# One copy of k and v out of PSUM: who frees the projection's bank in a hybrid decoder layer

## The chip, the cores and the metric

The kernel runs on one core of one Trainium2 chip. The metric is the device time of one execution in microseconds, from the kernel's first to its last work on the chip. Lower is better. The kernel before was run three times.

## The reference

The reference is one layer of a decoder in float32, for a prompt of 2048 tokens (with 16 learned tokens ahead of it) and 32 sample tokens (8 sequences of 4). Cut to what matters here:

```python
def in_project(h, g_pre, w_in):
    hn = rmsnorm(h, g_pre)
    proj = jnp.einsum('bsd,de->bse', hn, w_in)      # 1280 columns
    ...
    return q, k, v, u                               # 512, 128, 128, 512 columns

q, k = partial_rope(q, pos_p), partial_rope(k, pos_p)   # the first 16 of 64 columns of each head are rotated
att_o = swa_prompt(q, k, v, attn_sinks[l])              # window 128, blocks of 128, 8 heads of q, 2 of k and v
ssm_o, hr, hi = ssm_mixer(u, None, None, *ssm_p)        # complex state space, 32 groups
hp = hp + merge_out(att_o, ssm_o, ...)
hp = hp + sqrelu_mlp(hp, ...)
```

`partial_rope` rotates columns 0 to 7 against 8 to 15 of each head: x1 cos - x2 sin and x2 cos + x1 sin. The outputs are the layer's result for both kinds of tokens, the last 128 rows of k (rotated) and v, and the states of the state-space group.

## The kernel before, in words

The kernel has four stages: the u projection of all tokens with the preparation of the state-space tables (`phase_u`, to about 160 us of the span), attention and state space together (`phase_att`), the gated unit and the output projection (`phase_mix`), and the MLP (`phase_mlp`). All products are float32 by three matmuls: each operand is split into a high half, rounded by a ScalarE copy (`ACT.activation(..., AF.Copy)` into a float32r tile), and a low half, the difference (`split`, L93 to L99, and `mm3`, L108).

`phase_att` (L719) walks over 16 blocks of 128 tokens, `for i in range(NT)` at L993. A pass does, in the program's order: the scores of block i in two halves (`scores`, matmuls at L819, mask and maximum on VectorE at L824, exponentials on ScalarE at L830), the transposes of block i + 1's q and k (`tr`), the q, k and v projection of block i + 2 (`qkv_mm`, L436 and L437), one pair of the state-space groups (`s_rot`, `s_split`, `s_scan`, `s_hsplit`, `s_out`, `s_in`), the normalisation of the probabilities (L843, L845), their transposes with the split into PTh and PTl (`ptrans`, L847), `rope(i + 2)` between the two, the products with v (`pv`, `mm3` on PTh, PTl and v), and the split of block i + 3's x into axh and axl (`split_x`, the low half on GpSimd, L739). While this runs, GpSimd forms sums of MLP weights in `sums_step` (L1476 to L1479).

`rope` (L748) runs 17 times: for the 16 blocks and once, early, for the 48 sample and learned tokens (`rope(NT)`). It takes the two PSUM banks of the projection, `pq` (512 columns of q) and `pkv` (128 of k, 128 of v), and does in the kernel before:

- on ScalarE (ACT): the copy of k into columns 512 to 639 of the tile `qk`, scaled by the token's norm (L754); the copy of q into the first 512 (L755); the copy of v out of PSUM into its high half `vh` in the tile `v` (L759);
- on VectorE (DVE): the product with the cosines into the tile `ra` (L764), two products with the sines into `rb` (L765, L766), the sum of both back into `qk` (L767), and v's low half from PSUM, `vl` = v times norm less `vh` (L768);
- for the last block and the sample tokens also a plain copy of v out of PSUM into `vraw` (L771), and two DMAs from GpSimd's queue that store v and k (L773, L774; L776, L777). For the sample tokens VectorE splits `vraw` into `vns` (L778, L779).

So the bank of `pkv` is read by L754, L759, L768 and at times L771, and it is free for its next user when the last of them has read it.

PSUM has six banks for `mm_bank` and one tile of two banks, `b`, that the state-space products share (`b2_bank`, bufs=1). `s_in` (L905, 12 matmuls by `mm3` on sxh and sxl) can only write `b` when `s_out`'s result has been copied out by ACT at L960 (`sy`), and `s_out` when `s_rot` has read it (L920 to L922, VectorE).

The order in which an engine does its instructions isn't the program's. The kernel is built with a planner that places the instructions of every engine with a simulated timeline (`schedule_with_timeline_sim=True`, L1768): an instruction that is ready early in that model can be put ahead of one that stands before it in the program. Each engine then does its own list in order, and waits on semaphores for the others.

Of the kernel before, what the change touches and what calls it, by code (L numbers as in the profile page):

```python
# [8 lines left out]
F32 = mybir.dt.float32  # L9
F32R = mybir.dt.float32r  # L10
BF16 = mybir.dt.bfloat16
AF = mybir.ActivationFunctionType
OP = mybir.AluOpType
# [40 lines left out]
def ap(t, offset, dims):  # L54
    return bass.AP(tensor=t.tensor, offset=t.offset + offset, ap=[list(x) for x in dims])
# [3 lines left out]
def hymba_step(ctx: ExitStack, tc: tile.TileContext, A, O):  # L59
    nc = tc.nc  # L60
    PE, ACT, DVE, POOL, SP = nc.tensor, nc.scalar, nc.vector, nc.gpsimd, nc.sync
# [4 lines left out]
    def pool(stack, name, **kw):  # L66
        return stack.enter_context(tc.tile_pool(name=name, bufs=1, reuse_waits="tile", **kw))
# [7 lines left out]
    def mm_bank():  # L75
        return PS["pool"].tile([128, 512], F32, tag="mm", name="mm", bufs=PS["mm"])
# [4 lines left out]
    def r(t):  # L81
        return t.bitcast(F32)
# [52 lines left out]
    rstd = cst.tile([128, NT + 1], F32, name="rstd")  # L135
# [20 lines left out]
    def w_rows(ap_, k, c0, n):  # L156
        return ap_[k * 128:(k + 1) * 128, c0:c0 + n]

    # ------------------------------------------------------------------ u projection
    class Paced:  # L160
        def __init__(self, eng):
            self.eng = eng
# [556 lines left out]
    def phase_att(outer, eq, qw, QP, X01):  # L719
        with ExitStack() as es:  # L720
            cs, masks = AC["cs"], AC["masks"]
            pw = pool(es, "aw")
            wk = pool(es, "awork")
# [3 lines left out]
            vr = [pw.tile([128, 4, 2, 192], F32R, name=f"v{n}") for n in range(2)]  # L727
# [14 lines left out]
            def slot(i):  # L742
                return (i if i < NT else 3) % 4
# [4 lines left out]
            def rope(i):  # L748
                pq, pkv = QP.pop(i)
                n = 128 if i < NT else NX  # L750
                t = wk.tile([128, 10, 64], F32, name="qk", tag="qk", bufs=2)
                QK[i] = t
                tf = t.rearrange("p h d -> p (h d)")
                ACT.activation(tf[:n, 512:640], pkv[:n, :128], AF.Copy, scale=rstd[:n, i:i + 1])  # L754
                ACT.activation(tf[:n, :512], pq[:n], AF.Copy, scale=rq[:n, i:i + 1])  # L755
                s = slot(i)
                vp = pkv[:n, 128:256].rearrange("p (k d) -> p k d", k=2)
                vh, vl = (vr[m][:n, s, :, 64:128] for m in range(2))
                ACT.activation(vh, vp, AF.Copy, scale=rstd[:n, i:i + 1])  # L759
                c = cs[:n, i, 0, None, :].to_broadcast([n, 10, 16])  # L760
                sn = cs[:n, i, 1, None, :].to_broadcast([n, 10, 16])
                a = wk.tile([128, 10, 16], F32, name="ra", tag="ra", bufs=1)
                b = wk.tile([128, 10, 16], F32, name="rb", tag="rb", bufs=1)
                DVE.tensor_tensor(a[:n], t[:n, :, 0:16], c, op=OP.mult)  # L764
                DVE.tensor_tensor(b[:n, :, 0:8], t[:n, :, 8:16], sn[:, :, 0:8], op=OP.mult)  # L765
                DVE.tensor_tensor(b[:n, :, 8:16], t[:n, :, 0:8], sn[:, :, 8:16], op=OP.mult)  # L766
                DVE.tensor_tensor(t[:n, :, 0:16], a[:n], b[:n], op=OP.add)  # L767
                DVE.scalar_tensor_tensor(vl, vp, rstd[:n, i:i + 1], r(vh), op0=OP.mult, op1=OP.subtract)  # L768
                if i >= NT - 1:
                    v = wk.tile([128, 128], F32, name="vraw")  # L770
                    ACT.activation(v[:n], pkv[:n, 128:256], AF.Copy, scale=rstd[:n, i:i + 1])  # L771
                    if i < NT:
                        POOL.dma_start(O["v_p"], v)  # L773
                        POOL.dma_start(O["k_p"], t[:, 8:10, :].rearrange("p h d -> p (h d)"))  # L774
                    else:
                        POOL.dma_start(O["v_s"][:, 124:128, :], v[:NS])  # L776
                        POOL.dma_start(O["k_s"][:, 124:128, :], t[:NS, 8:10, :].rearrange("p h d -> p (h d)"))  # L777
                        DVE.tensor_copy(vns[:, 0], v[:n])  # L778
                        DVE.tensor_tensor(vns[:, 1], v[:n], r(vns[:, 0]), op=OP.subtract)  # L779
# [93 lines left out]
                    ACT.dma_start(ATD[:, :, :, 16 * i:16 * i + 16].rearrange("p k s c -> p (k s) c"),  # L873
                                  at.rearrange("p (a c) -> p a c", c=16))

            # state space: one pair of groups per step
            SX, SC, SS, SH = {}, {}, {}, {}
            wz = [pw.tile([128, 2, 2, 192], F32R, name=f"wz{n}") for n in range(2)]
            hst = pw.tile([128, 2, NCY], F32, name="hst")
# [101 lines left out]
            split_x(2)  # L981
            qkv(0)
            rope(0)
            tr(0)
            rope(NT)
            s_load(1)
            s_split(0)
            s_in(0)
            qkv(1)
            tr(NT)  # L990
            rope(1)
            nxt = 0
            for i in range(NT):  # L993
# [67 lines left out]
                load_a(i)  # L1061
                proj_a(i)

    # ------------------------------------------------------------------ gated unit, sample attention, output projection
    def advance(gen, n=1):
        for _ in range(n):
            next(gen, None)
# [101 lines left out]
        return 128 if i < NT else NS  # L1169

    def squares(pl, x, p, parts):
        """sums of squares over the four channel tiles: [channel, token]"""
        q = pl.tile([128, 4, 128], F32, name="pq", tag="pq", bufs=1)
        for k, s_ in parts:
            ACT.activation(q[:, k:k + s_.shape[1], :p], s_, AF.Square)
        q2 = pl.tile([128, 2, 128], F32, name="pq2", tag="pq2", bufs=1)
        POOL.tensor_tensor(q2[:, :, :p], q[:, 0:2, :p], q[:, 2:4, :p], op=OP.add)
        q3 = pl.tile([128, 128], F32, name="pq3", tag="pq3", bufs=2)
        POOL.tensor_tensor(q3[:, :p], q2[:, 0, :p], q2[:, 1, :p], op=OP.add)
        return q3  # L1180
# [216 lines left out]
        turn(ORD[NT])  # L1397
        return pre

    # ------------------------------------------------------------------ MLP  # L1400
    # Both products are cut in halves along tokens, contraction and result (Strassen-Winograd): seven products
    # of quarters each, with the sums of the activations' quarters formed in place and those of the weights' once.
    HN = (336, 352, 352)
    COL0 = (0, 672, 1376)
    ORDER = {"u": (1, 4, 6, 7, 5, 2, 3), "d": (4, 1, 6, 7, 5, 2, 3)}
# [82 lines left out]
    def phase_mlp(pre):  # L1488
        with ExitStack() as es:
# [5 lines left out]
            def add(out, a, b):  # L1495
                DVE.tensor_tensor(out, a, b, op=OP.add)  # L1496

            def combine(p, n, pt, q, both):
                """C11 = P1 + P2, C12 = P1 + P6 + P5 + P3, C21 = P1 + P6 + P7 - P4, C22 = P1 + P6 + P7 + P5"""
                if p == 1:  # L1500
                    ACT.activation(q[0], pt, AF.Copy)
                elif p == 4:
                    ACT.activation(q[2], pt, AF.Copy, scale=-1.0)
                elif p == 6:
                    add(q[1], q[0], pt)
                elif p == 7:
                    add(q[3], q[1], pt)
                    add(q[2], q[2], q[3])
                elif p == 5:
                    add(both, both, pt[:, None, :].to_broadcast([128, 2, n]))  # L1510
                elif p == 2:
                    add(q[0], q[0], pt)
                else:
                    add(q[1], q[1], pt)
# [31 lines left out]
                    combine(p, n, ACC["t"][t], q, Y[:, 4 + t, :2 * n].rearrange("p (i c) -> p i c", i=2))  # L1546

            def rows(c, p):
                """runs of up to 128 columns that hold tokens of one kind: (first column, number, rows of the output)"""
                out = []  # L1550
                while p:
                    j, x = divmod(c, 128)
                    n = min(p, 128 - x)
                    if j < NT:
                        r0 = 1024 * (j % 2) + j // 2 + 8 * x
                        dst = ap(O["y_p"], r0 * D, [[8 * D, n], [1, D]])
                    else:
                        dst = O["y_s"][x:x + n]
                    out.append((c, n, dst))
                    c, p = c + n, p - n  # L1560
                return out
# [35 lines left out]
                        end_b(*x, pt, c)  # L1597

            def end_a(c, n):
                """the first half of the features of the last tokens, scaled by the gain"""  # L1600
                f = M["H"].rearrange("p a c -> p (a c)")
                i = len(END)
                o = f[:, 1024 * i:1024 * i + 1024]
                h1 = f[:, 1024 * i + 3072:1024 * i + 4096] if i < 2 else mw.tile([128, D], F32, name="h1", tag="h1", bufs=1)
                SP.dma_start(h1[:n], H1D[COL0[2] + c:COL0[2] + c + n])
                st = mw.tile([128, 8], F32, name="est", tag="est", bufs=3)
                pt = mm_bank()[:n]
                for k in range(4):
                    PE.transpose(pt[:, 128 * k:128 * k + 128], Y[:, k, c:c + n], ident)
                sq = mw.tile([128, 512], BF16, name="esq", tag="esq", bufs=1)  # L1610
                ACT.activation(sq[:n], pt, AF.Square, accum_out=st[:n, 0:1])
                DVE.tensor_tensor(o[:n, :512], pt, gpost[:n, :512], op=OP.mult)
                END.append((o, h1, st))
# [159 lines left out]
```

## Time and profile before

| what | value |
|---|---|
| runs of the kernel before | 2208.49, 2202.45 and 2210.93 us, median 2208.49 us |
| span of the profiled execution | 2198.8 us, 37175 instructions |
| the profiled execution's own time | recorded by its span alone |
| PE (matmul) busy | 2083.1 us, 95% of the span |
| DVE, ACT, POOL busy | 1645.6, 1324.0 and 397.2 us |
| mean granted clock of PE | 0.970 of full speed |

PE is TensorE, DVE VectorE, ACT ScalarE, POOL GpSimd. The span goes from the first to the last instruction of one execution. "Busy" is the time in which an engine has an instruction under way; matmuls overlap, and their ends are modelled. A granted clock of 1.00 is the upper of TensorE's two levels, 2.4 GHz, and 0.50 the lower, 1.2 GHz. Busy shares over the whole span mix stages with different limits, so the tables that matter below are those of one stage.

### The profile page before, as it was taken

Reading aid. Unit: us, or ns where it says so; the run is one execution under the profiler, and the core shown is the slowest. Engines: PE = TensorE matmul, PEld = TensorE weight load, DVE = VectorE, ACT = ScalarE, POOL = GpSimd, SP = SyncE. Lnnn points to the kernel's source line nnn. Section 1 sums busy time; section 2 is a strip of 40 time slices with the busy share of each in tenths; the row PEclk is TensorE's granted clock in tenths of the full one; section 3 lists DMA queues with packets and bytes.
Section 4 is the critical chain, followed back from the end, with each engine's and each line's share of the span. In section 5 each row is a group of like instructions: output and inputs, shape, how many; then the busy total and the mean of one; then the engine's idle time right before and its main releaser. Section 6 shows DMA issues by size and latency. Waiting matters only on the chain.

```text
span 2198.8 us, 37175 instructions
## 1 busy us (share of the span) xinstructions
PE 2083.1 (95%) x12968; PEld 1963.3 (89%) x12968; DVE 1645.6 (75%) x3412; ACT 1324.0 (60%) x2877; POOL 397.2 (18%) x435
## 2 busy tenths in 40 slices
PE   7888999997799999989999999999999999999997
PEld 7877888786678787889999999999999999999995
DVE  8947788788678647469896885787868757787686
ACT  6644655555665545537865555588555555875555
POOL 5513545455142334000000000000000000000001
PEclk9998999998899999999999999999999999999999
DMA  8894666655577526778745465454454564444554
GB/s 291 240 222 117 158 183 169 166 155 158 168 224 256 184 85 209 221 240 287 246 144 144 136 189 184 139 191 135 137 143 149 176 181 138 158 135 140 134 161 151
DMA packets 351972, 387.16 MB, mean 176 GB/s; under 512 B 96504, under 2 KB 239512, under 8 KB 351768
## 3 DMA queue, kind: packets, MB, share of 16 engines
q1 hardware_dynamic: 285096, 378.13, 56.9%
q10 hardware_dynamic: 65792, 4.20, 1.8%
q0 software_dynamic: 896, 2.46, 0.4%
q8 instruction: 101, 1.65, 0.3%
q14 instruction: 87, 0.71, 0.1%
HBM read 303.26 MB, written 82.46 MB: 175 GB/s over the span
## 4 chain that ended last, share of the span: by engine, by line
PE 70%; DVE 10%; DMA 9%; ACT 4%; issue 4%; POOL 1%; SPq 1%; POOLq 0%; DVEq 0%; ACTq 0%
PE mm L111 20%; PE mm L110 20%; PE mm L112 20%; PE mm L436 2%; PE mm L819 2%; DMA Y<-in_w_down_dram 2%; PE mm L437 1%; DMA wr<-TU 1%; DVE e L843 1%; DMA zu<-YD 1%; DMA wt<-in_w_down_dram 1%; DVE wsl L96 1%; DVE e L824 1%; DMA qwr<-in_w_in_dram 1%; ACT e L845 1%
## 5 line engine op out<-in xcount | busy, mean ns | idle before, releaser
L111 PE MATMUL mm<-vl,wsh 128*128 128x352 f32 (+1 forms) x2624 | 839.9, 320 | 0.0
L110 PE MATMUL mm<-vh,wsh 128*128 128x352 f32 (+1 forms) x2624 | 839.3, 321 | 0.1
L112 PE MATMUL mm<-vh,wsl 128*128 128x352 f32 (+1 forms) x2624 | 816.4, 321 | 12.1 <-DVE wsl L96 11.9
L95 ACT ACTIVATE wsh<-wr 128x512 fp32r<-128x512 f32 x684 | 430.3, 629 | 440.0 <-PE mm L111 425.5
L96 DVE TENSOR_TENSOR wsl<-wr,wsh 128x512 fp32r<-128x512 f32 x684 | 471.4, 691 | 178.4 <-ACT wsh L95 177.4
L112 PEld LDWEIGHTS mm<-vh,wsl 128*128 128x128 f32 x2624 | 489.2, 188 | 15.5 <-DVE wsl L96 15.4
L110 PEld LDWEIGHTS mm<-vh,wsh 128*128 128x128 f32 x2624 | 494.6, 189 | 0.6 <-ACT wsh L95 0.4
L111 PEld LDWEIGHTS mm<-vl,wsh 128*128 128x128 f32 x2624 | 494.1, 188 | 0.0
L154 POOL TENSOR_TENSOR yst<-yst,nhalf 128x1 f32<-128x1 f32 (+2 forms) x15 | 13.4, 896 | 1250.1 <-DVE yst L153 1250.1
L1496 DVE TENSOR_TENSOR U<-U,mm 128x352 f32<-128x352 f32 (+3 forms) x240 | 140.1, 584 | 74.0 <-PE mm L112 73.4
L96 DVE TENSOR_TENSOR vl<-U,vh 128x352 fp32r<-128x352 f32 (+3 forms) x348 | 175.9, 507 | 1.6 <-ACT vh L95 1.0
L95 ACT ACTIVATE vh<-U 128x352 fp32r<-128x352 f32 (+3 forms) x348 | 162.9, 470 | 6.1 <-PE mm L111 5.9
L1529 ACT ACTIVATE U<-U 128x352 f32<-128x352 f32 (+1 forms) x192 | 92.9, 485 | 24.0 <-DVE U L1496 19.8
L1530 ACT ACTIVATE U<-U 128x352 f32<-128x352 f32 (+1 forms) x192 | 93.8, 490 | 4.4
L110 PE MATMUL mm<-xh,uwh 128*128 128x264 f32 (+1 forms) x256 | 73.4, 297 | 12.9 <-DVE U L528 7.0
L830 ACT ACTIVATE e<-e,mx 128x256 f32<-128x256 f32 x128 | 63.3, 498 | 33.0 <-DVE mx L827 32.7
L436 PE MATMUL mm<-qw,axh 128*128 128x512 f32 x224 | 78.9, 399 | 0.0
L111 PE MATMUL mm<-xl,uwh 128*128 128x264 f32 (+1 forms) x256 | 75.2, 297 | 0.0
L112 PE MATMUL mm<-xh,uwl 128*128 128x264 f32 (+1 forms) x256 | 73.0, 295 | 0.0
L764 DVE TENSOR_TENSOR ra<-qk,cs 128x160 f32<-128x160 f32 (+1 forms) x17 | 22.6, 1331 | 54.5 <-ACT qk L754 54.4
L819 PE MATMUL mm<-kT,qTh 64*128 64x256 f32 x256 | 54.4, 323 | 9.1 <-DVE v L768 9.1
L110 PEld LDWEIGHTS mm<-xh,uwh 128*128 128x128 f32 x256 | 50.1, 199 | 13.6 <-DVE U L528 7.5
(417 smaller groups left out, 4012.4 us busy)
## 6 DMA issues: line engine op xcount, KB each, us to landing
wr<-TU SPq DMA_DIRECT2D x192, 256.0 KB
wr<-TD SPq DMA_DIRECT2D x192, 256.0 KB
wr<-in_w_down_dram SPq DMA_DIRECT2D x156, 256.0 KB
wr<-in_w_up_dram SPq DMA_DIRECT2D x144, 256.0 KB
wt<-in_w_up_dram SPq DMA_DIRECT2D x32, 512.0 KB
TU<-wt SPq DMA_DIRECT2D x32, 512.0 KB
Y<-in_w_down_dram SPq DMA_DIRECT2D x20, 512.0 KB
TD<-Y SPq DMA_DIRECT2D x20, 512.0 KB
```

What stands on the lines that cost most here:

```text
L95: ACT.activation(hi, src, AF.Copy)
L96: (eng or DVE).tensor_tensor(lo, src, r(hi), op=OP.subtract)
L110: PE.matmul(out, ah, bh, start=start, stop=False)
L111: PE.matmul(out, ah, bl, start=False, stop=False)
L112: LAST[0] = PE.matmul(out, al, bh, start=False, stop=stop)
L436: PE.matmul(pq[:n], lh(k), rh[k][:, 0:512], start=st, stop=sp_)
L764: DVE.tensor_tensor(a[:n], t[:n, :, 0:16], c, op=OP.mult)
L819: PE.matmul(pts[kv][:, 256 * p:256 * p + 256], q, kTr[ki][sl, a:b + 1:b - a, :], start=(x == 0), stop=(x == 2))
L830: ACT.activation(e[:, u, j], e[:, u, j], AF.Exp, bias=mx[:, u, 1, j:j + 1], accum_out=mx[:, u, 3, j:j + 1])
L1496: DVE.tensor_tensor(out, a, b, op=OP.add)
L1529: ACT.activation(x, x, AF.Relu)
L1530: ACT.activation(x, x, AF.Square)
```

## The change

Only `rope` is changed. (Besides that the diff takes out or empties comment lines and docstrings.)

- `qk` grows from 10 to 12 heads of 64 columns. One ACT copy takes k and v together out of PSUM into columns 512 to 767, where L754 took k alone.
- v's high half is now a copy on ACT from `qk` in SBUF, and its low half a plain subtraction on GpSimd. VectorE's L768 goes.
- The product with the cosines is written in place into `qk`, behind the two products with the sines, and the tile `ra` goes.
- `vraw` and its copies L771 go: the last block and the sample tokens take v from `qk`.

```diff
-                t = wk.tile([128, 10, 64], F32, name="qk", tag="qk", bufs=2)
+                t = wk.tile([128, 12, 64], F32, name="qk", tag="qk", bufs=2)
                 QK[i] = t
                 tf = t.rearrange("p h d -> p (h d)")
-                ACT.activation(tf[:n, 512:640], pkv[:n, :128], AF.Copy, scale=rstd[:n, i:i + 1])
+                ACT.activation(tf[:n, 512:768], pkv[:n, :256], AF.Copy, scale=rstd[:n, i:i + 1])
                 ACT.activation(tf[:n, :512], pq[:n], AF.Copy, scale=rq[:n, i:i + 1])
-                s = slot(i)
-                vp = pkv[:n, 128:256].rearrange("p (k d) -> p k d", k=2)
-                vh, vl = (vr[m][:n, s, :, 64:128] for m in range(2))
-                ACT.activation(vh, vp, AF.Copy, scale=rstd[:n, i:i + 1])
                 c = cs[:n, i, 0, None, :].to_broadcast([n, 10, 16])
                 sn = cs[:n, i, 1, None, :].to_broadcast([n, 10, 16])
-                a = wk.tile([128, 10, 16], F32, name="ra", tag="ra", bufs=1)
                 b = wk.tile([128, 10, 16], F32, name="rb", tag="rb", bufs=1)
-                DVE.tensor_tensor(a[:n], t[:n, :, 0:16], c, op=OP.mult)
-                DVE.tensor_tensor(b[:n, :, 0:8], t[:n, :, 8:16], sn[:, :, 0:8], op=OP.mult)
-                DVE.tensor_tensor(b[:n, :, 8:16], t[:n, :, 0:8], sn[:, :, 8:16], op=OP.mult)
-                DVE.tensor_tensor(t[:n, :, 0:16], a[:n], b[:n], op=OP.add)
-                DVE.scalar_tensor_tensor(vl, vp, rstd[:n, i:i + 1], r(vh), op0=OP.mult, op1=OP.subtract)
+                DVE.tensor_tensor(b[:n, :, 0:8], t[:n, 0:10, 8:16], sn[:, :, 0:8], op=OP.mult)
+                DVE.tensor_tensor(b[:n, :, 8:16], t[:n, 0:10, 0:8], sn[:, :, 8:16], op=OP.mult)
+                DVE.tensor_tensor(t[:n, 0:10, 0:16], t[:n, 0:10, 0:16], c, op=OP.mult)
+                DVE.tensor_tensor(t[:n, 0:10, 0:16], t[:n, 0:10, 0:16], b[:n], op=OP.add)
+                s = slot(i)
+                vh, vl = (vr[m][:n, s, :, 64:128] for m in range(2))
+                ACT.activation(vh, t[:n, 10:12], AF.Copy)
+                POOL.tensor_tensor(vl, t[:n, 10:12], r(vh), op=OP.subtract)
                 if i >= NT - 1:
-                    v = wk.tile([128, 128], F32, name="vraw")
-                    ACT.activation(v[:n], pkv[:n, 128:256], AF.Copy, scale=rstd[:n, i:i + 1])
+                    v = t[:, 10:12].rearrange("p h d -> p (h d)")
```

## Rows read from the trace of the kernel before

**Rows 1.** Stage window: length, busy PE PEld DVE ACT POOL (counts), clock, DMA share, GB/s.

```profile
160.00:560.00 400.00, 359.51 (x2300) 309.43 (x2299) 320.12 (x864) 231.51 (x635) 198.57 (x207) 0.91 0.59 158
```

**Rows 2.** Waits of PE, 150 to 570 us: total us, times, longest.

```profile
PE mm L819 <- DVE v L768: 9.1, 8, 2.0
```

**Rows 3.** Timeline of ACT, 292.4 to 298 us: start, duration, line, out<-in, [idle before].

```profile
292.42 1.04 ACT L95 ACTIVATE axh<-axr 128x1024 fp32r<-128x1024 f32 x1
293.37 0.67 ACT L755 ACTIVATE qk<-mm,rq 128x512 f32<-128x512 f32 x1
293.94 0.35 ACT L754 ACTIVATE qk<-mm,rstd 128x128 f32<-128x128 f32 x1
...
295.39 0.64 ACT L960 ACTIVATE sy<-b 128x536 f32<-128x536 f32 x1
...
297.40 0.46 ACT L95 ACTIVATE cth<-sb 128x256 fp32r<-128x256 f32 x1
```

**Rows 4.** Timeline of POOL, 286 to 304 us.

```profile
293.54 2.35 POOL L96 TENSOR_TENSOR axl<-axr,axh 128x1024 fp32r<-128x1024 f32 x1 [3.56 <-ACT axh L95]
297.63 1.37 POOL L96 TENSOR_TENSOR sxl<-sx,sxh 128x552 fp32r<-128x552 f32 x1 [1.75 <-ACT sxh L95]
```

**Rows 5.** Timeline of DVE, 294 to 298 us.

```profile
294.32 1.75 DVE L764 TENSOR_TENSOR ra<-qk,cs 128x160 f32<-128x160 f32 x1 [3.49 <-ACT qk L754]
295.99 0.23 DVE L765 TENSOR_TENSOR rb<-qk,cs 128x80 f32<-128x80 f32 x1
...
296.30 0.34 DVE L768 SCALAR_TENSOR_TENSOR v<-mm,rstd,v 128x128 fp32r<-128x128 f32 x1
296.56 0.31 DVE L767 TENSOR_TENSOR qk<-ra,rb 128x160 f32<-128x160 f32 x1
```

**Rows 6.** Timeline of PE, at 296 and at 345 us.

```profile
296.69 0.50 PE L819 MATMUL mm<-kT,qTh 64*128 64x256 f32 x2 [1.22 <-DVE v L768]
...
297.68 0.60 PE L110 MATMUL b<-sxh,wz 128*128 128x276 f32 x1
...
345.58 0.50 PE L819 MATMUL mm<-kT,qTh 64*128 64x256 f32 x2 [1.24 <-DVE v L768]
```

**Rows 7.** Windows of PE alone: length, busy us (count), granted clock, DMA.

```profile
245.20:247.90 2.70, 0.38 (x1) 1.00 0.00 0
249.80:253.00 3.20, 3.20 (x15) 0.50 1.02 277
293.30:296.70 3.40, 0.43 (x3) 1.00 0.00 0
297.30:300.60 3.30, 3.30 (x16) 0.52 0.75 215
343.60:345.60 2.00, 0.46 (x3) 1.00 0.23 78
...
387.80:390.90 3.10, 0.38 (x1) 1.00 0.00 0
393.00:403.10 10.10, 10.10 (x44) 0.50 0.86 248
439.30:442.70 3.40, 0.64 (x2) 0.72 0.00 0
440.10:447.40 7.30, 5.28 (x20) 0.55 0.39 106
```

**Rows 8.** Instructions of line L1179: duration min/median/max in ns, forms.

```profile
L1179 POOL TENSOR_TENSOR pq<-pq x34: 451/463/3863, 512.2 to 856.9; 128x128 f32<-128x128 f32 x32, 128x32 f32<-128x32 f32 x2
```

**Rows 9.** Timeline of all engines, 159 to 176 us.

```profile
164.20 0.80 POOL L96 TENSOR_TENSOR ctl<-sb,cth 128x256 fp32r<-128x256 f32 x1
...
164.34 0.76 DVE L765 TENSOR_TENSOR rb<-qk,cs 128x80 f32<-128x80 f32 x1
```

**Rows 10.** Timeline of PE, 319 to 321 us.

```profile
319.62 0.39 PE L110 MATMUL b<-sxh,wz 128*128 128x276 f32 x1 [0.41 <-ACT sy L960]
...
320.86 0.29 PE L110 MATMUL b<-sxh,wz 128*128 128x276 f32 x1
```

## The prediction

> **What bounds the kernel now.** I first read the table by stage, to see where the touched code runs and how much room is there. The touched function `rope` runs 17 times, all in the stage from 160 to 560 us. There PE is busy 360 of 400 us, at a granted clock of 0.91 [rows 1]. So all that can be won or lost lies in one fifth of the span: some 40 us of idle PE, and the clock.
>
> Next I read who PE waited for in that stage. In 8 passes it waited for L768, the DVE instruction that makes v's low half out of PSUM: 9.1 us in all [rows 2]. Often it has waited for ACT's PTh copies just before.
>
> Then I followed the pass around 294 us engine by engine. ACT splits the next x (axh, to 293.46) and then makes the copies of `rope`: L755, L754, which ends at 294.29, and L759 [rows 3]. POOL starts axl when axh is done and holds on until 295.89 [rows 4]. DVE's first rope instruction, L764, starts at 294.32 and needs 1.75 us; L765, of half its size, takes 0.23 [rows 5]. L764 ends 0.2 us behind axl: it stood behind POOL. L768 therefore ends only at 296.64. The score matmuls (L819) want the PSUM bank that k and v are still read from, and start 0.05 us later, after 1.22 us of idle PE [rows 6]. So a short DVE job holds a bank because of the four that stand around it on a blocked engine.
>
> Last I read PE's clock around these waits. In four of the steady passes PE is idle, busy time taken off the window, for 2.32, 2.97, 2.72 and 2.76 us, and each time the granted clock falls, in that place or soon after it, to its lower level, 1.2 GHz, for 3 to 10 us. Around 345 us PE is idle for 2.00 - 0.46 = 1.54 us, and the clock stays at 2.4 GHz [rows 7].
>
> **Part by part.** *ACT.* The copy of k grows from 128 to 256 columns. L754 and L755 give 0.35 us at 128 and 0.67 at 512 columns, 0.83 ns a column, so 0.46 at 256. L759, from PSUM and of L754's size, becomes a copy of 128 columns from SBUF. Axh (1.04 at 1024) and cth (0.46 at 256) give 0.76 ns a column, so 0.36 at 128 [rows 3]. ACT thus pays 0.11 us more a rope. Whether a copy that reads what ACT has just written starts later is shown nowhere. Consecutive copies overlap by 0.10 us, so between 0 and 0.10; I take 0, since L755 or a PTh copy can stand between. ACT sets the PTh wait, and 13 of the ropes lie in the steady passes: 1.4 us lost. The two copies L771 go; they stand where nothing waits.
>
> *DVE.* L764 to L767 stay four instructions of the same shapes, in another order; the in-place product has the size of L764. L768 goes. DVE's instructions overlap, so it is worth 296.56 - 296.30 = 0.26 us a rope [rows 5]. The first rope instruction will still stand behind axl, as L764 does.
>
> *POOL.* It gets one subtraction of 128x128 more a rope. The like shape at L1179 takes 0.46 us [rows 8]. Axl is followed by 1.7 us in which POOL waits for the next sxh, so it has room, and what is queued behind it (sxl, and then ctl) waits for ACT's later copies anyhow. The v of rope(i + 2) is read two passes on, some 45 us later, so nobody waits for it. The subtraction and DVE's rope do read SBUF at the same time. From below it costs DVE nothing. From above it holds one rope instruction for its 0.46 us, as at 164 us, where L765 took 0.76 with POOL's ctl copies beside it, not 0.23 [rows 5, 9]. I take 0.26, what L768 gives back, because a hold-up ends with the instruction that causes it and DVE has the order on its side in part. The four POOL DMAs of k and v stay four; v's now read `qk` itself, whose tiles k's DMAs hold already. The tiles `ra` and `vraw` go, `qk` grows by 128 columns: no wait hangs on them.
>
> *The wait.* The bank is now freed by the wide copy, at about 294.4 in the pass shown, before the PTh copy that PE waits for first. So L768's wait goes everywhere. What is late next? In five of the eight passes (one of them is in the rows) the state-space input (L110 on sxh) stands behind the scores; it needs the bank that ACT's sy empties at 296.03 [rows 3, 6], which is before it could start even then. There the wait counts in full: 0.76 + 1.22 + 1.22 + 1.23 + 1.02 = 5.4 us. In the other three, DVE's PTl or the state-space rotation is due right behind the scores, on DVE, and it comes no earlier than DVE does: 0.26 us each, 0.8 us, which the subtraction takes again by the value above. That makes 5.4 - 1.4 = 4.0 us.
>
> *The clock.* Less the waits, and with ACT's 0.11 more, the idle sums of the four steady places become 1.2, 1.9, 1.6 and 1.9 us [rows 7]. The row with 1.54 kept the clock, and its longest single piece was 1.24 [rows 6]. With L768's wait gone the PTh wait is one piece, and only the first place stays under 1.24. So I let that one drop go, whose stretch at the lower level costs 3.20 x (1 - 0.50) = 1.6 us, and keep the other three. From below nothing is won (0); from above all four go: 1.6 + 1.6 + 5.0 + 3.3 = 11.5 us, each its stretch by what the clock lacks to 1.
>
> **Sum.** 4.0 + 1.6 = 5.6 us off. The profiled execution has a span of 2198.8 us; what of its own time lies around the span isn't recorded, and the median of the three runs is 9.7 us above it. I take that part as unchanged: 2208.5 - 5.6, about 2203 us.
>
> **Rivals.** *A: the clock stays up in all four places.* For it: as sums, all four lie nearer to 1.54, which kept the clock, than to 2.32, the least that lost it. Against: in one piece, three of them are longer than any that kept it. 4.0 + 11.5 = 15.5 us off: 2193 us.
>
> *B: POOL's subtraction eats the gain.* POOL reads SBUF in it, and each rope instruction of DVE reads two SBUF tiles. If it always holds DVE for 0.46 us, and DVE's PTl decides in all 13 passes, that is 13 x (0.46 - 0.26) = 2.6 us lost; with ACT's extra 0.10 for reading its own result 1.3 us more; and the clock drops all stay. 4.0 - 2.6 - 1.3 = 0.1: 2208 us. The Trainium skill, in "SBUF — State Buffer", section "Who interferes with whom", speaks for this: a VectorE instruction with two SBUF inputs is fully blocked by a GpSimd instruction that reads SBUF, for the length of that instruction, and one with a single SBUF input isn't. By that rule the change swaps an instruction that is never blocked (L768 reads PSUM) for one that blocks. L764's 1.75 us agrees. Which of the two starts first decides who is held, and no row here shows that for the new pair.
>
> *C: slower, by the planned order.* The instructions of each engine are put in order at build time by a planner that runs a model of the times, so a new release time can change places. In six passes the 12 matmuls of the state-space input now stand ahead of PV and fill PE's wait (at 319.62 they start as soon as sy is done). If the planner, now that the scores can go early, puts them behind, PE stands idle for the time that they take, 12 x (320.86 - 319.62) / 9 = 1.65 us [rows 10], longer, and a drop of the clock follows, on average 11.5 / 4 = 2.9 us: 4.5 us a pass. One such pass outweighs the 4.0 us; four of the six give 18.0 - 4.0 = 14.0 us more: 2222 us. Against: the same planner has put them ahead wherever sy was early enough.
>
> That the change doesn't do what it says is excluded for the bank: only the wide copy reads k and v's PSUM.
>
> **How the numbers follow.** A difference of 0.5% is about what a measurement of this kernel can tell from none: 11 us, so below 2197.4 and above 2219.5. The forecast gets 0.45, A 0.23, B 0.20, C 0.12. Faster by over 0.5%: A, and the part of the forecast in which the long stretch at 393 us goes as well (0.07): 0.30. Slower: C with four passes or more, 0.09. The rest is 0.61. The range goes from 2190, just beyond A, to 2217, about three passes of C (2208.5 + 13.5 - 4.0 = 2218).
>
> **What would show it.** The waits of PE for L768 must be gone, and none for the wide copy in their place. PE's remaining waits must be for PTh, at most 0.11 us longer. ACT's wide copy should take 0.46 us and POOL's subtraction 0.46, in POOL's pause behind axl. DVE's first rope instruction should still end with axl. The stretch at the lower clock around 250 us should be missing. I am wrong if PE waits for something else in the same places for as long (then the order or B), if the stage's clock goes clearly above 0.91 (A), or if PE's gaps appear in passes that had none (C).

## The result and the profile after

Eight runs of each kernel stand against each other: 2206.40 us before in the median (2201.91 to 2210.93; the three runs made first are among them), 2214.35 us after (2210.43 to 2222.69). The ratio is 1.0052, with a 95% interval from 1.0034 to 1.0071. The changed kernel is slower by about 11 us (0.0052 x 2206), where 5.6 us less had been forecast; the time lies inside the range that was given, on the other side of no change.

The profiled execution of the changed kernel has a span of 2219.5 us (its own time was 2221.26 us, 6.9 above the median, so the two profiles lie 20.7 us apart and the runs only 11; the lines after L763 have moved up by three). The table of its stages answers to [rows 1]:

```profile
160.00:560.00 400.00, 363.58 (x2266) 313.36 (x2265) 314.19 (x818) 224.38 (x613) 200.51 (x216) 0.89 0.57 154
```

PE is busier there than before and yet does less: 2266 matmuls, not 2300, at a clock of 0.89 and not 0.91. The last copy of an attention result (`at`) starts at 581.9 us, before at 564.0, and from there to the end the two profiles take 1637.6 and 1634.8 us. So the loss is made in this stage.

The waits of PE in the passes, from 176 to 540 us, answer to [rows 2]:

```profile
PE mm L110 <- ACT PTh L95: 10.5, 9, 1.9
PE mm L111 <- DVE PTl L96: 6.5, 5, 2.7
PE b L110 <- ACT sy L957: 1.0, 1, 1.0
```

The wait of the scores for v is gone, and none for the wide copy came in its place. But PE waits 6.5 us for PTl, which it didn't in the kernel before, and longer for PTh, where the kernel before has

```profile
PE mm L110 <- ACT PTh L95: 6.9, 6, 1.8
```

The instructions of the change, by line, with minimum, median and maximum in ns:

```profile
L754 ACT ACTIVATE qk<-mm,rstd x15: 454/461/473, 185.0 to 525.4; 128x256 f32<-128x256 f32 x15
L765 ACT ACTIVATE v<-qk x15: 300/313/338, 185.6 to 526.2; 128x128 fp32r<-128x128 f32 x15
L766 POOL TENSOR_TENSOR v<-qk,v x15: 452/456/477, 186.0 to 526.8; 128x128 fp32r<-128x128 f32 x15
L759 DVE TENSOR_TENSOR rb<-qk,cs x15: 243/1564/1902, 185.5 to 525.9; 128x80 f32<-128x80 f32 x15
L760 DVE TENSOR_TENSOR rb<-qk,cs x15: 228/493/759, 185.7 to 526.1; 128x80 f32<-128x80 f32 x15
```

The wide copy and the subtraction have the size that was worked out (0.46 us each); the copy from SBUF takes 0.31 us, less than the 0.36 that were put in. The first rope instruction, now L759, ends with axl as L764 did [rows 4, 5], and the second, held by the new subtraction, takes 0.49 us where the row of L765 had 0.23.

The longest wait for PTl is at 234 us. Timelines of DVE, POOL and PE there:

```profile
228.25 2.96 DVE L921 TENSOR_TENSOR sz<-sz,sq 128x258 f32<-128x258 f32 x2
231.12 0.77 DVE L759 TENSOR_TENSOR rb<-qk,cs 128x80 f32<-128x80 f32 x1
231.82 0.76 DVE L760 TENSOR_TENSOR rb<-qk,cs 128x80 f32<-128x80 f32 x1
232.62 0.47 DVE L761 TENSOR_TENSOR qk<-qk,cs 128x160 f32<-128x160 f32 x1
233.12 0.73 DVE L762 TENSOR_TENSOR qk<-qk,rb 128x160 f32<-128x160 f32 x1
233.77 1.87 DVE L96 TENSOR_TENSOR PTl<-mm,PTh 128x512 fp32r<-128x512 f32 x3
...
228.52 2.39 POOL L96 TENSOR_TENSOR axl<-axr,axh 128x1024 fp32r<-128x1024 f32 x1 [4.63 <-ACT axh L95]
230.87 0.93 POOL L96 TENSOR_TENSOR ctl<-sb,cth 128x256 fp32r<-128x256 f32 x1
231.76 0.72 POOL L96 TENSOR_TENSOR ctl<-skt,cth 128x256 fp32r<-128x256 f32 x1
232.45 0.45 POOL L766 TENSOR_TENSOR v<-qk,v 128x128 fp32r<-128x128 f32 x1
232.86 0.80 POOL L96 TENSOR_TENSOR wz<-sb,wz 128x256 fp32r<-128x256 f32 x1
...
234.50 0.58 PE L111 MATMUL mm<-PTl,v 128*128 128x256 f32 x1 [2.69 <-DVE PTl L96]
```

In this pass DVE does the state-space rotation and then the rope, one instruction for each of POOL's, and PTl stands behind both. PE's clock falls right behind. PE's idle time there, 0.35 + 2.69 = 3.04 us, is about the widest sum before (2.97 us at 293 us), though the widest single piece before, the wait for e aside, is 1.97 us. The stretches at the lower level are more, and longer in total: eight, and before five, without the last two of each kernel, which lie at the end of the passes in all of them. Five of the eight, in windows of PE alone, answer to [rows 7]:

```profile
203.00:217.00 14.00, 12.65 (x50) 0.51 0.50 152
234.00:245.00 11.00, 10.50 (x44) 0.53 0.41 127
281.00:289.00 8.00, 6.75 (x27) 0.57 0.48 111
309.00:323.00 14.00, 14.00 (x61) 0.51 0.71 200
360.00:368.00 8.00, 6.78 (x32) 0.57 0.76 194
```

Each length times what the clock lacks to 1, summed over these stretches of the passes ("lost clock" from here on), gives 32.4 us, and 18.8 us in the kernel before. The last two, left out here and in the table below, add 8.5 to 13.6 us to each kernel; with them it is 42.7 and 30.7 us. A stretch counts whole, with the time in it in which PE is idle.

The start of the stage is longer, too. PE stands still from 163.7 to 173.1 us; DVE and POOL there:

```profile
168.23 4.64 DVE L776 TENSOR_TENSOR vns<-qk,vns 48x128 fp32r<-48x128 f32 x1
172.79 0.16 DVE L919 COPY fins<-b 128x16 f32<-128x16 f32 x1
172.88 0.30 DVE L762 TENSOR_TENSOR qk<-qk,rb 128x160 f32<-128x160 f32 x1
...
168.25 0.87 POOL L766 TENSOR_TENSOR v<-qk,v 128x128 fp32r<-128x128 f32 x2
169.07 1.34 POOL L96 TENSOR_TENSOR sxl<-sx,sxh 128x552 fp32r<-128x552 f32 x1
170.38 2.33 POOL L96 TENSOR_TENSOR axl<-axr,axh 128x1024 fp32r<-128x1024 f32 x1
```

One DVE instruction with two SBUF operands is held through four POOL instructions without a gap, two of them new, and fins and the rope's sum, for which PE waits, are queued behind it.

### The profile page after: what moved, and what is told of

The parts are those of the page before. It is cut to its first block, busy times and chain, and to the rows that moved or that the text cites. A ratio compares the mean times of both kernels' runs of the same rounds, so it can differ in the third digit from the quotient of the medians.

```text
span 2219.5 us, 37163 instructions
## 1 busy us (share of the span) xinstructions
PE 2092.3 (94%) x12968; PEld 1970.2 (89%) x12968; DVE 1653.7 (75%) x3395; ACT 1326.8 (60%) x2875; POOL 402.1 (18%) x452
## 4 chain that ended last, share of the span: by engine, by line
PE 66%; DVE 10%; DMA 6%; ACT 4%; issue 3%; POOL 1%; SPq 0%; POOLq 0%; ACTq 0%; DVEq 0%
PE mm L111 20%; PE mm L110 20%; PE mm L112 20%; DMA Y<-in_w_down_dram 3%; PE mm L816 2%; PE mm L436 1%; DVE e L840 1%; DVE e L821 1%; DVE wsl L96 1%; DMA zu<-YD 1%; PE mm L437 1%; ACT e L842 1%; DMA wt<-in_w_down_dram 1%; PE b L1567 1%; DVE sg L928 0%
## 5 line engine op out<-in xcount | busy, mean ns | idle before, releaser
L112 PEld LDWEIGHTS mm<-vh,wsl 128*128 128x128 f32 x2624 | 488.7, 188 | 19.8 <-DVE wsl L96 19.8
L827 ACT ACTIVATE e<-e,mx 128x256 f32<-128x256 f32 x128 | 63.5, 501 | 18.4 <-DVE mx L824 18.2
L110 PE MATMUL mm<-oh,psh 128*128 128x512 f32 (+1 forms) x136 | 57.0, 419 | 4.9 <-ACT zt L1115 3.3
L110 PE MATMUL mm<-oh,pah 128*128 128x512 f32 (+1 forms) x136 | 56.1, 418 | 5.3 <-ACT oh L98 5.3
```

Of the source, the lines that this page charges most:

```text
L110: PE.matmul(out, ah, bh, start=start, stop=False)
L112: LAST[0] = PE.matmul(out, al, bh, start=False, stop=stop)
L827: ACT.activation(e[:, u, j], e[:, u, j], AF.Exp, bias=mx[:, u, 1, j:j + 1], accum_out=mx[:, u, 3, j:j + 1])
```

## The experiments

The planner had put more than the touched lines in another order. To separate order from work, most of these kernels have the order of each engine's list fixed: a table gives the place of every listed instruction, and each is tied to the one ahead of it by an order without a wait. In short:

```diff
     hymba_step(tc, args, outs)
+    _in_order(tc, nc, _mybir)
...
+    for n in places:                      # one list for each engine
+        tc.add_manual_dep(by[e][n], was.name, NoSync, reason="order")
+        was = by[e][n]
```

All ratios are to runs of the kernel before on the same chip; experiments 1 to 3, 4 to 7, 8 to 11 and 12 with 13 had a chip each, so small differences between these groups say little. "Start" is from the first copy of q to the first score product, "passes" from there to the last `at`, both of the profiled execution; the waits are PE's from 176 to 540 us, in which the slower kernels do a little less of their work. In the second experiment the 19.0 us are waits of the scores that end with a PTl. In the lists below sxl, ctl and wz are low halves of state-space operands, which GpSimd forms as it forms axl; fins is a copy of the state-space result on VectorE, and e the exponentials of the scores.

| kernel | ratio [95%] | start | passes | lost clock | waits v / PTl / PTh |
|---|---|---|---|---|---|
| before | 1 | 18.5 | 383.2 | 18.8 | 9.1 / 0 / 6.9 |
| after | 1.0052 [1.0034, 1.0071] | 22.1 | 396.3 | 32.4 | 0 / 6.5 / 10.5 |
| 1 after, order of before | 0.9999 [0.9982, 1.0016] | 22.7 | 383.2 | 18.8 | 0 / 2.3 / 8.2 |
| 2 before, order of after | 1.0136 [1.0109, 1.0162] | 24.1 | 412.5 | 49.5 | 0 / 19.0 / 5.0 |
| 3 after, vns moved | 1.0053 [1.0034, 1.0072] | 21.7 | 391.2 | 25.6 | 0 / 5.7 / 8.8 |
| 4 as 1, subtraction on DVE | 0.9977 [0.9962, 0.9992] | 19.0 | 382.7 | 22.2 | 0 / 1.5 / 8.6 |
| 5 as 1, subtraction late | 1.0007 [0.9992, 1.0021] | 22.9 | 383.6 | 20.5 | 0 / 2.8 / 7.1 |
| 6 start before, rest after | 1.0037 [1.0020, 1.0054] | 18.4 | 393.8 | 29.0 | 0 / 6.6 / 9.2 |
| 7 start after, rest before | 1.0003 [0.9987, 1.0019] | 23.5 | 383.9 | 20.5 | 0 / 2.8 / 8.1 |
| 8 as 1, first two late | 0.9995 [0.9981, 1.0009] | 19.8 | 383.4 | 22.2 | 0 / 3.0 / 5.8 |
| 9 after, rope behind PTl | 0.9996 [0.9981, 1.0011] | 23.3 | 381.4 | 22.2 | 0 / 0.7 / 10.1 |
| 10 as 4, rope behind PTl | 0.9959 [0.9944, 0.9973] | 19.5 | 373.4 | 10.2 | 0 / 1.8 / 9.3 |
| 11 before, two lines swapped | 1.0000 [0.9984, 1.0015] | 17.0 | 381.3 | 18.8 | 9.3 / 0 / 6.7 |
| 12 before, rope behind PTl | 0.9952 [0.9935, 0.9968] | 19.7 | 370.4 | 8.6 | 0.2 / 1.3 / 8.5 |
| 13 as 1, rope behind PTl | 0.9969 [0.9955, 0.9984] | 20.4 | 379.6 | 15.4 | 0 / 0.8 / 10.9 |

The passes are 370 to 413 us long in these fifteen profiles, but less their lost clock all of them take 359 to 366 us: by length they differ almost only by the time at the lower level. The runs' mean granted clock over the whole span goes the same way: 0.965 in the median after and 0.959 in experiment 2, 0.970 or 0.971 in the runs of the kernel before, and 0.974 to 0.976 in experiments 10, 12 and 13.

**1 and 2: work and order apart.** The lists of the other kernel are given to each.

```diff
-PE, DVE, ACT, POOL, SP: the planner's lists
+the lists of the other kernel (what only one of the two has stays free)
```

> The changed work with every engine's list in the order that the kernel before has: TensorE's and SyncE's lists are identical to it, the other lists but for the instructions that the change adds or drops. Theory T1 (the order that the planner chose for the changed kernel makes the loss, the work does not): no slower than the kernel before, 2195 to 2208 us, and the two waits of TensorE for v gone, as forecast. Theory T2 (the work makes the loss: the subtraction on GpSimd and the two-operand SBUF instructions of VectorE hold each other up, and ScalarE's longer copies delay PTh): it keeps most of the loss, 2212 to 2220 us.

> The work of the kernel before in the order that the changed kernel has (TensorE's and SyncE's lists identical to that one). T1: it gets slower, 2212 us or more, since it also keeps its waits for v. T2: within 4 us of the kernel before, 2203 to 2211 us.

The first is level with the kernel before, the second 1.4% slower. With the old order the loss is gone: the order makes it, not the work. The second says less than it was meant to. L768, which only the old work has, was free there, and the planner put it behind the rope and one to three PTl; and PE waits at the scores (13 waits, 19.0 us in all), which in the changed kernel with the same list it doesn't. These waits end with a PTl, and the eleven longest of them before L768 has ended, so those aren't for v's bank; what the scores wanted there stays open. PE and DVE at the longest:

```profile
233.75 0.79 PE L819 MATMUL mm<-kT,qTh 64*128 64x256 f32 x2 [3.52 <-DVE PTl L96]
...
236.32 0.34 DVE L768 SCALAR_TENSOR_TENSOR v<-mm,rstd,v 128x128 fp32r<-128x128 f32 x1
```

But the first also lacks the gain. Waits of PE in its passes:

```profile
PE mm L110 <- ACT PTh L95: 8.2, 6, 1.9
PE mm L849 <- DVE e L840: 5.8, 1, 5.8
PE b L110 <- ACT sy L957: 2.6, 4, 1.5
PE mm L111 <- DVE PTl L96: 2.3, 3, 1.2
PE b L110 <- DVE fins L919: 1.7, 1, 1.7
```

9.1 us of waits for v have gone, and 1.3 (PTh), 1.6 (sy), 2.3 (PTl) and 1.7 us (fins) have come. Without the wait for e, which belongs to the last passes, all waits together are 17.2 us before and 16.0 here.

**3: the held instruction at the start.**

```diff
 L760 TENSOR_TENSOR rb<-qk,cs 128x10x8
-L775 CAST vns<-qk 48x128
...
-L776 TENSOR_TENSOR vns<-qk,vns 48x128
...
 L762 TENSOR_TENSOR qk<-qk,rb 48x10x16
+L775 CAST vns<-qk 48x128
+L776 TENSOR_TENSOR vns<-qk,vns 48x128
```

> The changed kernel in its own order, with the two instructions that make the sample tokens' copy of v (lines 775 and 776) moved behind the rope of the extra tokens on VectorE, and nothing else moved. If the subtraction of line 776, which took 4.64 us there beside GpSimd's run of subtractions, is what holds TensorE at the start of the stage: 3 to 4.5 us faster than the changed kernel, 2209 to 2212 us, and the pause of TensorE at 164 us falls from 9.3 to about 5.7 us. If GpSimd's run holds whatever VectorE does next (the lock, not the instruction): the rope's sum or the copies behind it are held as long, the pause stays over 8 us and the time within 1.5 us of the changed kernel.

The second case, by the time: with L776 away, the next instruction with two SBUF operands was held as long, and the start shrank only from 22.1 to 21.7 us. PE's pause didn't stay in one piece of over 8 us, though; it became two waits, 4.9 us for fins and 3.0 for the rope's sum.

```profile
165.44 4.75 DVE L762 TENSOR_TENSOR qk<-qk,rb 128x160 f32<-128x160 f32 x1
```

**4, 5 and 8: what GpSimd's subtraction costs.** All have the order of the kernel before.

```diff
-                POOL.tensor_tensor(vl, t[:n, 10:12], r(vh), op=OP.subtract)
+                DVE.tensor_tensor(vl, t[:n, 10:12], r(vh), op=OP.subtract)     # 4
...
 axl                                                                            # 5, POOL's list
-vl
 sxl, ctl, ctl, wz
+vl
...
-vl, vl                                                                         # 8, block 0 and extra tokens
 wz, sxl, axl, ctl, ctl
+vl, vl
```

> The changed work with the subtraction that makes v's lower half on VectorE instead of GpSimd, every list in the order of the kernel before (the subtraction stands where line 768 stood). In the first experiment the change in that order gained nothing: TensorE's waits for v were gone, but 3.5 us were lost at the start of the stage and as much as the waits had cost came back as waits for PTh, PTl, sy and fins. Theory B (GpSimd's new subtraction takes the gain, by holding VectorE's rope): the pause of TensorE at 164 us falls from 7.5 to about 5.7 us, the second rope instruction from 0.49 to 0.23 us, and the time is 3 to 6 us below the kernel before (ratio 0.997 to 0.9985). Theory D (TensorE is held to the pace of VectorE and ScalarE in these places whatever reads v, so that the removed wait comes back as the next one): ratio 0.9985 to 1.001.

> The changed work in the order of the kernel before, with GpSimd's subtractions of blocks 2 to 14 moved four or five places back, behind the state-space splits of the same pass (sxl, ctl and wz); the start is as in the first experiment. Theory B: the second rope instruction falls from 0.49 to 0.23 us, sy and fins come sooner, TensorE's waits of the steady passes fall by 2 us or more, and the time by 2 to 4 us against the first experiment (ratio to before 0.998 to 0.9995). Theory D: within 1.5 us of the first experiment.

> The kernel of the first experiment (the changed work in the order of the kernel before) with GpSimd's first two subtractions, those of block 0 and of the extra tokens, moved from ahead of wz, sxl and axl to behind them; nothing else moved. If these two keep GpSimd's run without a gap, so that the rope's sum of block 0 (4.07 us in the first experiment, 0.31 with the subtraction on VectorE) finds no place before axl is done: the sum takes under 1 us, TensorE's pause at 164 us falls from 7.5 to about 4.5 to 5.7 us, and the time comes to 0.997 to 0.999 of the kernel before. If the place on VectorE's side is what mattered in the fourth experiment (the subtraction there as a stop between the two): the sum is held 2 us or more and the ratio stays 0.999 to 1.0015.

The fourth gains 0.23%, about 5 us (1.8 to 8.4 by its interval). In the steady passes the subtraction isn't what matters: in the fifth L760 was back at 0.23 us, the waits fell from 16.0 to 14.8 us, less than the 2 us expected, and the time did not fall. At the start the profiles show a price. The rope's sum of block 0, first in the first experiment, then in the fourth with POOL's axl beside it, then in the eighth:

```profile
166.23 4.07 DVE L762 TENSOR_TENSOR qk<-qk,rb 128x160 f32<-128x160 f32 x1
```

```profile
167.17 0.31 DVE L762 TENSOR_TENSOR qk<-qk,rb 128x160 f32<-128x160 f32 x1
...
167.41 2.37 POOL L96 TENSOR_TENSOR axl<-axr,axh 128x1024 fp32r<-128x1024 f32 x1 [0.17 <-ACT axh L95]
```

```profile
166.85 1.10 DVE L762 TENSOR_TENSOR qk<-qk,rb 128x160 f32<-128x160 f32 x1
```

The two subtractions ahead of sxl and axl make POOL late, so that axl follows sxl with no gap; without them axl has to wait for axh, and the sum goes in between. The start shrank by 3.7 us in the fourth and by 2.9 in the eighth. Whether the eighth's time fell with it can't be told: its interval spans both the first's and a gain of 0.19%. So the place of the price is read from profiles only; no run's time shows it, and the seventh, with a start of 23.5 us, is level with the kernel before. The sum was expected under 1 us and the pause at 5.7 at most; 1.10 and 6.1 us were measured (PE's wait for that sum).

**6 and 7: which part of the order.**

```diff
-lists of the changed kernel
+the first some 1,700 places from one kernel, the rest in the order of the other
```

> The changed work, in the order of the kernel before up to the first score product (some 1,700 instructions of all engines) and in the changed kernel's own order behind it. If the new order at the start of the stage makes the loss: ratio to before 1.000 to 1.002. If the order of the steady passes does: ratio 1.004 to 1.007, as the changed kernel, with TensorE's waits for PTl (6.5 us there) and the added stretches at the lower clock still in it.

> The reverse: the changed work in its own order up to the first score product, in the order of the kernel before behind it. If the order of the start makes the loss: ratio to before 1.004 to 1.006. If that of the steady passes does: 1.000 to 1.0015 (the start costs at most the 1.2 us by which its first scores come later than in the first experiment).

The steady passes make the loss: 1.0037 with the new order there (just under the 1.004 expected), 1.0003 with it at the start alone, although that start is 23.5 us long.

**9 and 10: the rope behind PTl.** DVE's list alone is edited, in blocks 2 to 15.

```diff
-L759, L760, L761, L762                       # in 10 with L766
 PTl, PTl
+L759, L760, L761, L762
```

> The changed kernel in its own order, with VectorE's four rope instructions of blocks 2 to 15 moved from ahead of the first two PTl of the pass to behind them; nothing else moved. If the place of the rope, held by axl, ahead of PTl is what the new order costs in the steady passes: TensorE's waits for PTl fall from 6.5 to under 2 us, fewer stretches at the lower clock follow, and the ratio to before falls from 1.004 to 1.005 to between 0.999 and 1.002. If the order costs by its other places (TensorE's own list): PTl's waits turn into others and the ratio stays at 1.003 or more.

> The kernel of the fourth experiment (subtraction on VectorE, order of the kernel before, ratio 0.9977) with the rope's four instructions and the subtraction moved behind the first two PTl of the pass in blocks 2 to 15. If the rope's hold-up by axl still costs there: the waits for PTl (1.5 us), fins and sy (1.6 us each) fall and the ratio is 0.9955 to 0.9975. If in this order only PTh, which ScalarE makes, ends the waits: 0.997 to 0.9985.

This one move takes back as much as the new order lost: 0.9996, passes 14.9 us shorter, lost clock 22.2 us in place of 32.4. PE's own list hasn't changed, so it doesn't make the loss by itself. But that the rope stands ahead of PTl isn't new: in the old order, too, it stands ahead of the pass's first PTl in all 14 passes, as here in the first experiment:

```profile
225.03 1.58 DVE L759 TENSOR_TENSOR rb<-qk,cs 128x80 f32<-128x80 f32 x1 [3.72 <-ACT qk L754]
...
227.50 0.33 DVE L762 TENSOR_TENSOR qk<-qk,rb 128x160 f32<-128x160 f32 x1
227.75 1.28 DVE L96 TENSOR_TENSOR PTl<-mm,PTh 128x512 fp32r<-128x512 f32 x2
```

And the same move gains in the old order as well: 0.30% from experiment 1 to 13 (0.9999 to 0.9969), 0.56% here (1.0052 to 0.9996). With the move in both, 0.27% is left between the two orders (0.9996 and 0.9969), at the edge of what the intervals separate. So the rope's place need not be all of the difference; what else makes it isn't shown. In the tenth the waits for fins and sy fell by 0.6 and 0.8 us against the fourth, but those for PTl and PTh grew by 0.3 and 0.7: 13.3 us in all and 13.5, without e. The gain is the clock's: 10.2 us lost and not 22.2.

**11: a null change.**

```diff
-                ACT.activation(tf[:n, 512:640], pkv[:n, :128], AF.Copy, scale=rstd[:n, i:i + 1])
                 ACT.activation(tf[:n, :512], pq[:n], AF.Copy, scale=rq[:n, i:i + 1])
+                ACT.activation(tf[:n, 512:640], pkv[:n, :128], AF.Copy, scale=rstd[:n, i:i + 1])
```

> The kernel before with its two copies of lines 754 and 755 written in the other order in the program: the same work, planned anew. Theory T1 says that a new plan alone can move the time by as much as the change did; here TensorE's list differs in some sixty places from the one before, so a ratio anywhere from 0.997 to 1.005 would agree, and one that leaves 1.000 by more than its interval would show it. If plans of the same work are worth the same: 0.9985 to 1.0015.

A new plan that differs in few places is worth the same. It doesn't speak for T1.

**12 and 13: is it the change at all?**

```diff
+L768                                          # 12, the kernel before; 13: L759 to L762 of the changed one
-L764, L765, L766, L768, L767
 PTl, PTl
+L764, L765, L766, L767
```

> The kernel before, its own work and order, with the rope's four instructions (764 to 767) of blocks 2 to 15 moved behind the first two PTl of the pass, so that line 768, which gives the bank back, comes before all of them and isn't behind axl any more. No part of the change is in it. If the gain of the tenth experiment (0.9959) is the order's and not the change's: TensorE's waits for v fall from 9.1 to under 2 us and the ratio is 0.995 to 0.9975. If the change is needed for it (the bank given back by ScalarE's copy): the waits for v stay over 4 us, since line 768 still follows both copies and v's upper half, and the ratio is 0.9985 to 1.0015.

> The tenth experiment with the subtraction on GpSimd, as the change has it (the changed work, the order of the kernel before, the rope behind the first two PTl). If GpSimd's subtraction costs by its hold on the rope while the rope stands ahead of PTl and at the start: with the rope out of the way only the start is left, ratio 0.9965 to 0.9985, TensorE's pause at 164 us near 7.5 us again. If it costs beyond that: ratio 0.9985 or more. If it costs nothing: 0.995 to 0.9965, with the pause under 6 us.

The kernel before with this move is the fastest of all, 0.9952, with none of the change in it; the tenth, with the change's early release of the bank and the same move, is level with it. One pass of DVE in the twelfth, and the stretches at the lower clock in its passes, again without the last two:

```profile
336.54 0.35 DVE L768 SCALAR_TENSOR_TENSOR v<-mm,rstd,v 128x128 fp32r<-128x128 f32 x1 [4.37 <-ACT v L759]
337.02 0.69 DVE L96 TENSOR_TENSOR PTl<-mm,PTh 128x512 fp32r<-128x512 f32 x1
...
338.92 0.68 DVE L96 TENSOR_TENSOR PTl<-mm,PTh 128x512 fp32r<-128x512 f32 x1
339.52 0.63 DVE L764 TENSOR_TENSOR ra<-qk,cs 128x160 f32<-128x160 f32 x1
340.07 0.77 DVE L765 TENSOR_TENSOR rb<-qk,cs 128x80 f32<-128x80 f32 x1
340.76 0.78 DVE L766 TENSOR_TENSOR rb<-qk,cs 128x80 f32<-128x80 f32 x1
```

```profile
221.00:225.00 4.00, 4.00 (x20) 0.57 0.55 137
245.00:249.00 4.00, 4.00 (x19) 0.57 0.64 163
293.00:297.00 4.00, 4.00 (x20) 0.57 0.82 223
344.00:348.00 4.00, 4.00 (x21) 0.57 0.95 290
385.00:389.00 4.00, 4.00 (x21) 0.57 0.79 182
```

L768 needs 0.35 us and comes as soon as ACT's copy is done; the bank and the first two PTl no longer wait behind the rope, which POOL still holds (0.77 us for L765, not 0.23). Lost clock is 20.00 x (1 - 0.57) = 8.6 us, less than half of what it was. The thirteenth gives 0.9969, and 0.9959 without GpSimd's subtraction in the tenth: the 0.1% between them the intervals don't separate from nothing. The ratio lies in the range of the first case; PE's pause at 164 us, 6.5 us, lies between the two.

One thing wasn't tried: TensorE's list of one kernel with VectorE's list of the other. So what each of the two adds to the order's loss stays open.

## Why the prediction was wrong

*The wait.* Right in its first half: L768's waits went everywhere, the wide copy has the forecast size, and no wait for it came. "What is late next" was sized at 5.4 us won, 1.4 lost. In the order of the kernel before and without GpSimd's subtraction (experiment 4) the waits of the passes, without e, fell from 17.2 to 13.5 us, 3.7 won for the 4.0 forecast, and the time by about 5 us for the 5.6 forecast. That the times agree is partly luck: the profiled passes there are no shorter than before, since the clock took back what the waits gave (below). The price of ACT's longer copies (1.4 us) isn't confirmed by PTh's 1.7 us more: with the measured 0.31 us the copies cost 0.07 us a rope (0.46 + 0.31 - 0.70), 0.9 in all, and with the same copies PTh's waits are 8.2, 7.1 and 5.8 us in experiments 1, 5 and 8.

*The order.* The step that failed: the durations were put into the old order, and the new order got a chance of 0.12, as rival C, for one place only (the state-space input behind PV). The order did change and made the time slower, but elsewhere. PE now waits 5 times, 6.5 us in all, for PTl, which stands behind the rope that POOL holds, and at 234 us behind the state-space rotation as well. Experiments 1, 6, 7 and 9 show the order as the cause: ratio 0.9999 with the old order, the loss in the steady passes and not at the start, and 0.9996 when the rope alone is moved. Since the rope stands ahead of PTl in the old order too, and moving it gains 0.30% there, other places of the new order must turn it into a loss. Which they are stays open.

*The clock.* One drop less, 1.6 us, was forecast. In the changed kernel 13.6 us more were lost (32.4 - 18.8; 12.0 with the last two stretches), and that is about all of the 13.1 us by which its passes are longer; its waits, without e, are 18.4 us to 17.2. In experiment 4 it was 3.4 us more (22.2 - 18.8): the stretch around 250 us, which was to go, is 15 us long there (246 to 261 us) and not 4. So this step failed in the old order too, and the profiled passes there are no shorter than before (382.7 and 383.2 us). Where the 5 us of its runs lie, one profiled execution doesn't tell. The forecast also left out the longest stretch of the kernel before, 198 to 213 us, 6.8 us of lost clock behind the 1.97 us wait for L768: only four of the five were priced.

*GpSimd's subtraction.* It was priced at 0.26 us a rope, by the steady passes. The size is right (L760 takes 0.49 us, not 0.23), and there it costs nothing that can be measured (experiment 5). What the step left out is the start of the stage, where POOL's list has no room: 4.2 us more in the profile of experiment 1, of which experiment 4 gives back 3.7. So rival B probably named the part that eats the gain in the old order (0.9999 with it, 0.9977 without, intervals that still overlap), but not the place, which the profiles alone show. The rule of the Trainium skill that spoke for it ("SBUF — State Buffer", section "Who interferes with whom": the second of the two to issue is blocked until the first has finished) agrees with L760's 0.49 us; at the start the hold was longer than any single instruction of POOL, 4.07 us against axl's 2.4, so the prediction's sentence that a hold-up ends with the instruction that causes it doesn't hold there.

*What the profile of before already showed.* L764's 1.75 us beside L765's 0.23 [rows 5] was read as the reason for L768's lateness, and then the change was costed as if the bank were the matter. Experiment 12 shows that it was what stood ahead in the queue: with the rope behind L768 and PTl, L768's waits fall from 9.1 to 0.2 us and the kernel gains 0.48%, without the change. How much of that comes from L768's place and how much from PTl's wasn't tried apart. With the same move the change adds nothing: 0.9969 as it stands, 0.9959 with the subtraction on VectorE, 0.9952 without it.

## What to carry to other kernels

When the instruction that an engine is waited for is short, look at what stands ahead of it in its queue and move that, before rewriting the instruction. Where a planner orders the lists, a forecast by durations holds only for the order it was read from: time a change once in the old order, fixed by hand, and once as planned, and the two parts show. A GpSimd instruction added for "free" had no price here where GpSimd had a gap behind it; look for its price where GpSimd's run has none.

## What the runs showed of the hardware

- An instruction of VectorE with two SBUF operands can be held through several GpSimd instructions without a gap between them: L776 4.64 us, L762 4.75 and 4.07 us, against 0.30 us for L762 unheld. With a gap of 0.17 us in GpSimd's run the sum took 0.31 us. It isn't always so: at 231 us in the changed kernel the rope's four instructions pass one by one beside ctl, ctl, the subtraction and wz, 0.47 to 0.77 us each, with no gap between those either. What decides it isn't shown.
- Waits of the same total can cost very different clock. In experiments 4 and 10 PE waits 13.5 and 13.3 us in the passes, without e, and loses 22.2 and 10.2 us to the lower level: stretches of 4 to 15 us in the one, all of 4 us in the other (the last two of each left out).
- Two orders of the same work, the old one, differ by 1.8% here: 0.9952 in experiment 12 and 1.0136 in experiment 2. In the passes nearly all of it is lost clock: 8.6 and 49.5 us, for passes of 370.4 and 412.5 us.
